# Norming the attention latents with tokens in the rows, and fixing TensorE's order, in a hybrid attention and convolution layer

## The chip, the cores and the metric

The kernel runs on one core of a Trainium2 chip. The metric is the device time of one execution in microseconds (us), the median over runs. One profiled execution gives the trace that the text reads. Engines are named as in the profile: PE is TensorE (PEld its weight loads), DVE is VectorE, ACT is ScalarE, POOL is GpSimd, and SP is SyncE, whose queue issues most of the DMAs.

## What is computed

One decoder layer on 256 tokens of 2048 float32 features. The input is normed, projected into ten parts, run through multi-head latent attention and a short gated convolution, and merged. The reference, cut to what matters here:

```python
h = _rmsnorm(x, pre_norm_g)
proj = jnp.einsum('bsd,de->bse', h, w_in)
(q_a, c_kv, k_rope, z_mla, c_in, b_gate, c_gate, z_conv,
 g_mla, g_conv) = jnp.split(proj, cuts, axis=-1)      # 512, 512, 64, then 2048 each

q = jnp.einsum('bsr,re->bse', _rmsnorm(q_a, q_a_norm_g), w_q_b)      # 16 heads of 128 + 64
kv = jnp.einsum('bsr,re->bse', _rmsnorm(c_kv, kv_a_norm_g), w_kv_b)  # 16 heads of 128 + 128
q_rope = _apply_rope(q_rope, cos, sin); k_rope = _apply_rope(k_rope, cos, sin)
attn = _causal_mla_attention(q_nope, q_rope, k_nope, k_rope, v)
y_mla = einsum(attn * silu(z_mla), w_o_mla)
u = c_gate * c_in; conv = causal 3-tap convolution of u
y_conv = einsum(b_gate * conv * silu(z_conv), w_o_conv)
merged = sigmoid(g_mla) * y_mla + sigmoid(g_conv) * y_conv
x = x + _rmsnorm(einsum(merged, w_out), post_norm_g)
```

`_rmsnorm(x, g)` is `x * rsqrt(mean(x*x) + eps) * g`. The norm of x is one factor per token, so the kernel projects the raw `x * g` and multiplies by that factor afterwards.

## The kernel before

**Numbers.** Every float32 operand of a large product is kept as a high and a low part in a matmul format (fp32r). ScalarE makes the high part (`split_act`, L211), VectorE the remainder (L212), and a product is taken as three matmuls: high x high, high x low, low x high. Where activations are the moving operand, high and low stand side by side in 512 columns (`halves`, L206: weight high times both; L208: weight low times the high 256). Where activations are stationary, `product` (L198 to L200) issues the three.

**Weights.** They come in units of 1 MB (128 x 2048), in the order of a list, `plan`. `load_raw` (L141) issues a unit on SyncE into one of three buffers `raw`; `split_unit` makes `whi` and `wlo` halves of 128 x 1024, five buffers each; `take(i)` splits one unit ahead and loads two more.

**Stages.** First the transposed input `xt` is loaded in pieces between the units of the q latent and split into `x_both` (L281, L282), which holds it with features in the rows for the whole kernel. The q latent (`qa`) takes four units and the four blocks of the c_kv latent (`ckv`) one each; both come out of TensorE with latent features in the rows and tokens in the columns, and `whole` (L329, L330) adds the two halves of a PSUM bank. Then comes the key's rope part (`kr`, L424). For the norms, `squares` squares on ScalarE (L293) and reduces on VectorE (L295), `rms_cols` sums over rows with a matmul against ones (L303), takes the power -1/2 on GpSimd (L310) and builds diagonal matrices (L314), and `rms_rows` spreads them over all rows with another matmul (L321). This is done for x, for q and for c_kv. `times_rows` and `latent_split` then scale and split. `tables` (L342 to L372) reduces the rotary angles on GpSimd in some 35 steps (L348 to L360, then pairs of L352 and L353), and VectorE and ScalarE make sine and cosine.

**Heads.** For each of 16 heads five projections of x follow, z, cg, ci, b and c (`project`), with the gates and the convolution, the scores after z (`scores`), the transposes of the softmax weights `p` after ci (`turn`, L522), the product with v after b (`values`), and, for the next pair of heads, `group_a` (query and key, after the first head of a pair) or `group_b` (query rope and v, after the second). In head 0 all groups, the scores, `turn` and `values` stand at the end. After the heads, four chunks of output columns: two gates, two products, a merge on VectorE (L655 to L660), and `features` (L633), which transposes the merged chunk with TensorE. The output product and the last norm end the kernel.

**Order.** The program runs under a tile scheduler that simulates the engines and picks, on each engine, the first ready instruction in program order; one that it thinks not ready may be passed by later ones. `tc.keep_in_program_order(i)` ties an instruction behind the one before it on its engine in the program.

Of the kernel before, what the change touches and what calls it, by code (L numbers as in the profile page):

```python
# [78 lines left out]
def tile_layer(ctx: ExitStack, tc: tile.TileContext, xt, x, pos, pvec, post_g, wqa, wi, wkr, wqk, wrv, wsq, out):  # L79
    nc = tc.nc  # L80

# [24 lines left out]
    u_qa = [add(wqa[k]) for k in range(4)]  # L106
    u_ckv = [add_wi() for _ in range(KR)]
# [87 lines left out]
    def product(ps, a, b, first, last):  # L195

        (ah, al), (bh, bl) = a, b
        nc.tensor.matmul(ps, ah, bh, start=first, stop=False)  # L198
        nc.tensor.matmul(ps, ah, bl, start=False, stop=False)  # L199
        nc.tensor.matmul(ps, al, bh, start=False, stop=last)  # L200

    def halves(blocks):


        for ps, w, both, first, _ in blocks:
            nc.tensor.matmul(ps[:, :], w[0], both, start=first, stop=False)  # L206
        for ps, w, both, _, last in blocks:
            nc.tensor.matmul(ps[:, :S], w[1], both[:, :S], start=False, stop=last)  # L208
# [24 lines left out]
    for _ in range(8):  # L233
        nc.tensor.matmul(idle[:, :P], ones[:, :], ones[:, :], start=True, stop=True)
# [4 lines left out]
    r_col = const.tile([P, LINE], F32, name="r_col")[:, :NT]  # L239
# [13 lines left out]
    kr = bp.tile([P, 2, S], F32R, name="kr")  # L253
    mask = bp.tile([P, 3 * P], F32, name="mask")
# [4 lines left out]
    xs = at_f  # L259
    angles = [at_f[:, H - 1 - i, :] for i in range(5)]  # L260
    lat_f = {"qa": cv_f[:, :KR, :], "ckv": cv_f[:, KR : 2 * KR, :]}
    sq_f = cv_f[:, 8:12, :]
    acc_f = {"x": cv_f[:, 12, :], "qa": cv_f[:, 13, :], "ckv": cv_f[:, 14, :]}
    row_f = at_f[:, 10, :]
    kr_f, kr_g = cv_f[:, 15, :], at_f[:, 9, :]
# [23 lines left out]
    def squares(name, chunks):  # L289

        acc = acc_f[name]
        for i, src in enumerate(chunks):
            nc.scalar.activation(sq_f, src, AF.Square)  # L293
            part = temp("f")[:, :] if i else acc
            nc.vector.reduce_sum(part, sq_f.rearrange("p k t -> p t k"), axis=mybir.AxisListType.X)  # L295
            if i:
                nc.vector.tensor_tensor(acc, acc, part, op=ALU.add)
        return acc

    def rms_cols(name, acc, width, r=None):  # L300
        ss = bank(f"ss_{name}", tag="sm", bufs=1)
        for t in range(NT):
            nc.tensor.matmul(  # L303
                ss[:, t : t + 1], acc[:, t * P : (t + 1) * P], ones[:, 0:1], start=True, stop=True
            )
        v = temp(f"v_{name}", (P, NT), tag="rms_v")
        nc.vector.tensor_scalar(v[:, :], ss[:, :NT], 1.0 / width, EPS, op0=ALU.mult, op1=ALU.add)
        if r is None:
            r = temp(f"r_{name}", (P, NT), tag="rms_r")
        nc.gpsimd.tensor_tensor(r[:, :], v[:, :], mhalf[:, :].to_broadcast([P, NT]), op=ALU.pow)  # L310
        dgs = []
        for t in range(NT):
            dg = temp(f"dg_{name}{t}", (P, P), tag=f"rms_d{t}", bufs=1)
            nc.vector.tensor_scalar(dg[:, :], ident[:, :], r[:, t : t + 1], None, op0=ALU.mult)  # L314
            dgs.append(dg)
        return dgs

    def rms_rows(name, dgs, r):
        rb = bank(f"rb_{name}", tag="sm", bufs=1)
        for t in range(NT):  # L320
            nc.tensor.matmul(rb[:, t * P : (t + 1) * P], ones[:, :], dgs[t][:, :], start=True, stop=True)  # L321
        nc.scalar.activation(r, rb[:, :S], AF.Copy)
        return r
# [18 lines left out]
    def tables():  # L342
        pi = angles[4].bitcast(I32)
        nc.scalar.dma_start(out=pi, in_=pos.to_broadcast([P, S]))
        y, n1, n2, r = angles[:4]
        v = nc.gpsimd
        nc.vector.tensor_copy(y[:, :], pi)
        v.tensor_scalar(r[:, :], y[:, :], col("freq"), None, op0=ALU.mult)  # L348

        def less(r, n, c):  # L350

            v.tensor_scalar(y[:, :], n[:, :], c, None, op0=ALU.mult)  # L352
            v.tensor_tensor(r[:, :], r[:, :], y[:, :], op=ALU.subtract)  # L353
# [3 lines left out]
        v.tensor_scalar(y[:, :], r[:, :], inv, None, op0=ALU.mult)  # L357
        v.tensor_scalar(n1[:, :], y[:, :], big, big, op0=ALU.add, op1=ALU.subtract)
        v.tensor_tensor(n2[:, :], y[:, :], n1[:, :], op=ALU.subtract)
        v.tensor_scalar(n2[:, :], n2[:, :], small, small, op0=ALU.add, op1=ALU.subtract)  # L360
        for w, c in TERMS:
            less(r, (n1, n2)[w], c)
        v.tensor_scalar(n1[:, :], r[:, :], inv, small, op0=ALU.mult, op1=ALU.add)
        v.tensor_scalar(n1[:, :], n1[:, :], small, None, op0=ALU.subtract)
        for c in COARSE:
            less(r, n1, c)
        lim = float(np.nextafter(np.float32(math.pi), np.float32(0)))
        nc.vector.tensor_scalar(r[:, :], r[:, :], lim, -lim, op0=ALU.min, op1=ALU.max)
        nc.vector.scalar_tensor_tensor(y[:, :], r[:, :], -1.0, r[:, :], op0=ALU.mult, op1=ALU.max)
        nc.scalar.activation(n2[:, :], r[:, :], AF.Sin)  # L370
        nc.scalar.activation(cos_t[:, :], y[:, :], AF.Sin, bias=hpi[:, :], scale=-1.0)
# [12 lines left out]
    def times_rows(dst):  # L384
        n = dst.shape[1]
        nc.vector.tensor_tensor(dst, dst, r_x[:, :].unsqueeze(1).to_broadcast([P, n, S]), op=ALU.mult)

    def latent_split(name, both, g, r):
        f = lat_f[name]
        for j in range(KR):  # L390
            nc.vector.scalar_tensor_tensor(
                f[:, j, :], f[:, j, :], col(g, j), r, op0=ALU.mult, op1=ALU.mult
            )
            split_act(both[:, j, :S], both[:, j, S:], f[:, j, :])

    pss = [bank(f"qa{j}") for j in range(KR)]
    for i in range(4):
        ahead(u_qa[i], split=0)
        for k in range(4 * i, 4 * i + 4):
            behind = split_scaled(x_both, xs[:, k, :], k)  # L400
        w = take(u_qa[i])
        for k4 in range(4):
            k = 4 * i + k4
            halves([(pss[j], w(k4 * KR + j, P), x_both[:, k, :], k == 0, k == KD - 1) for j in range(KR)])
    for j in range(KR):
        whole(lat_f["qa"][:, j, :], pss[j])
    with tc.issue_after(behind[0].ins), tc.issue_after(behind[1].ins):
        squares("x", [xs[:, 4 * i : 4 * i + 4, :] for i in range(4)])
    whole(lat_f["ckv"][:, 0, :], project(u_ckv[0], "ckv0", tag="tp", bufs=1))
    dg = rms_cols("x", acc_f["x"], D, r_col)  # L410
    whole(lat_f["ckv"][:, 1, :], project(u_ckv[1], "ckv1"))
    rms_rows("x", dg, r_x[:, :])
    times_rows(lat_f["qa"])
    squares("qa", [lat_f["qa"]])
    whole(lat_f["ckv"][:, 2, :], project(u_ckv[2], "ckv2"))
    whole(lat_f["ckv"][:, 3, :], project(u_ckv[3], "ckv3"))
    dg = rms_cols("qa", acc_f["qa"], R)
    times_rows(lat_f["ckv"])
    squares("ckv", [lat_f["ckv"]])
# [3 lines left out]
    for k in range(KD):  # L423
        nc.tensor.matmul(ps[:, :], w[k // 8][:, k % 8], x_both[:, k, :], start=k == 0, stop=k == KD - 1)  # L424
# [4 lines left out]
    latent_split("qa", qa, "q_g", rms_rows("qa", dg, row_f))  # L429
    tables()  # L430
# [31 lines left out]
    def group_b(g):  # L462
# [8 lines left out]
        for t in range(NT):  # L471
            ps = bank(f"vv{g}_{t}", **({} if g else {"tag": ("o", "tp")[t], "bufs": 1}))
# [6 lines left out]
    def scores(h):  # L479
# [5 lines left out]
        mm = nc.tensor.matmul  # L485
# [32 lines left out]
    def turn(h, p):  # L518

        tp = bank(f"tp{h}", tag="tp", bufs=1)  # L520
        for b in range(3):
            nc.tensor.transpose(tp[:, b * P : (b + 1) * P], p[:, b * P : (b + 1) * P], ident[:, :])  # L522
# [4 lines left out]
    def values(h, pt, sz):  # L527
# [5 lines left out]
        mm = nc.tensor.matmul  # L533
# [7 lines left out]
    def silu(name, ps):  # L541
        f, s = temp("sl_f", bufs=1), temp(name, bufs=1)
# [12 lines left out]
    for h in range(H):  # L555
        uz, ug, ui, ub, uc = u_head[h]
        sz = silu("sz", project(uz, f"z{h}"))
        if h == 0:
            dg_c = rms_cols("ckv", acc_f["ckv"], R)
            key_rope()  # L560
        else:
            p = scores(h)
# [3 lines left out]
        if h == 0:  # L566
            latent_split("ckv", ckv, "kv_g", rms_rows("ckv", dg_c, row_f))
# [5 lines left out]
        if h > 0:  # L573
            pt = turn(h, p)
        c = temp("c", bufs=1)
# [52 lines left out]
    def features(c, m):  # L628

        for t in range(NT):  # L630
            tp = bank(f"mt{c}_{t}", tag=("tp", "o")[t], bufs=1)
            for j in range(4):
                nc.tensor.transpose(tp[:, j * P : (j + 1) * P], m[t][:, j * P : (j + 1) * P], ident[:, :])  # L633
# [176 lines left out]
```

## Time and profile before

| | |
|---|---|
| median of 3 runs | 1073.79 us (1073.71 to 1073.86) |
| the profiled execution | 1074.65 us |
| its span in the trace | 1072.9 us |
| granted TensorE clock, mean | 0.995 |
| busy in the span: PE, PEld, DVE, ACT, POOL | 1054.6, 909.6, 728.8, 587.2, 48.0 us |
| moved by DMA | 199.80 MB, 186 GB/s in the mean |

Busy time is what the profiler shows per engine. Matmuls are pipelined, so one's length (about 390 ns for 512 columns) is more than the distance to the next (about 230 ns); distances are read from the starts. "Idle before" is the time in which an engine sat still before an instruction, and the name behind the arrow is what ended it.

### The profile page before, as it was taken

How to read it: one execution, taken by the hardware profiler on the slowest of the kernel's cores; microseconds unless marked ns; L12 is line 12 of the kernel's file. 1: busy time of each engine (PE TensorE's matmuls, PEld its weight loads, DVE VectorE, ACT ScalarE, POOL GpSimd, SP SyncE). 2: the span in 40 equal slices, each digit the busy share in tenths (PEclk: the TensorE clock that was granted, in tenths of full speed). 3: DMA queues.
4: the chain of work that ended last, by engine and by line, in shares of the span. 5: the costliest groups of instructions: out<-in, count | busy, mean ns of one | idle time of the engine just before them, and what ended most of it. 6: DMA issues, size and time to landing. Idle time of an engine off the chain costs nothing.

```text
span 1072.9 us, 14367 instructions
## 1 busy us (share of the span) xinstructions
PE 1054.6 (98%) x5576; PEld 909.6 (85%) x5576; DVE 728.8 (68%) x1132; ACT 587.2 (55%) x849; POOL 48.0 (4%) x70
## 2 busy tenths in 40 slices
PE   9989999999999999999999999999999999999997
PEld 7878798988988888889888878888888888888885
DVE  6899797777877878778787684454454445455562
ACT  7656566666666666666666664434434433434450
POOL 0591000000000000000000000000000000000000
PEclk9999999999999999999999999999999999999999
DMA  8644454454554545554545536555555555557552
GB/s 313 223 147 161 148 192 167 177 196 148 196 197 152 192 164 188 188 177 168 187 162 194 194 114 239 196 196 183 188 191 184 195 196 196 196 192 284 199 188 78
DMA packets 31604, 199.80 MB, mean 186 GB/s; under 512 B 3632, under 2 KB 5296, under 8 KB 9264
## 3 DMA queue, kind: packets, MB, share of 16 engines
q1 hardware_dynamic: 30960, 195.57, 51.8%
q10 hardware_dynamic: 576, 3.31, 0.8%
q8 instruction: 43, 0.70, 0.3%
q14 instruction: 25, 0.20, 0.1%
HBM read 196.78 MB, written 2.10 MB: 185 GB/s over the span
## 4 chain that ended last, share of the span: by engine, by line
PE 86%; DVE 5%; POOL 4%; issue 2%; DMA 2%; ACT 0%; SPq 0%; POOLq 0%; DVEq 0%; ACTq 0%
PE sq L199 10%; PE sq L200 10%; PE sq L198 10%; PE z L206 5%; PE cg L206 5%; PE ci L206 5%; PE c L206 5%; PE b L206 5%; PE c L208 3%; PE b L208 3%; PE z L208 3%; PE ci L208 3%; PE cg L208 3%; PE out L200 2%; PE out L198 2%
## 5 line engine op out<-in xcount | busy, mean ns | idle before, releaser
L212 DVE TENSOR_TENSOR wlo<-raw,whi 128x1024 fp32r<-128x1024 f32 (+1 forms) x372 | 442.6, 1205 | 230.2 <-ACT whi L211 192.7
L211 ACT ACTIVATE whi<-raw 128x1024 fp32r<-128x1024 f32 (+1 forms) x374 | 386.8, 1038 | 339.8 <-PE sq L200 181.3
L199 PE MATMUL sq<-wlo,x_both 128*128 128x512 f32 x256 | 99.7, 390 | 1.6 <-DVE wlo L212 1.6
L200 PE MATMUL sq<-whi,x_both 128*128 128x512 f32 x256 | 99.6, 389 | 0.0
L198 PE MATMUL sq<-whi,x_both 128*128 128x512 f32 x256 | 99.2, 390 | 0.0
L206 PE MATMUL z<-x_both,whi 128*128 128x512 f32 x256 | 62.7, 398 | 2.4 <-DVE f L330 2.4
L206 PE MATMUL ci<-x_both,whi 128*128 128x512 f32 x256 | 62.9, 398 | 0.0
L206 PE MATMUL b<-x_both,whi 128*128 128x512 f32 x256 | 62.2, 395 | 0.0
L206 PE MATMUL cg<-x_both,whi 128*128 128x512 f32 x256 | 61.3, 391 | 0.0
L206 PE MATMUL c<-x_both,whi 128*128 128x512 f32 x256 | 61.1, 391 | 0.0
L206 PEld LDWEIGHTS z<-x_both,whi 128*128 128x128 f32 x256 | 48.2, 193 | 12.2 <-issue 2.6
L199 PEld LDWEIGHTS sq<-wlo,x_both 128*128 128x128 f32 x256 | 48.1, 188 | 11.8 <-DVE wlo L212 2.0
L200 PEld LDWEIGHTS sq<-whi,x_both 128*128 128x128 f32 x256 | 48.1, 188 | 10.0
L198 PEld LDWEIGHTS sq<-whi,x_both 128*128 128x128 f32 x256 | 48.1, 188 | 9.9
L206 PEld LDWEIGHTS ci<-x_both,whi 128*128 128x128 f32 x256 | 48.0, 193 | 9.4
L206 PEld LDWEIGHTS c<-x_both,whi 128*128 128x128 f32 x256 | 47.0, 188 | 9.1
L206 PEld LDWEIGHTS cg<-x_both,whi 128*128 128x128 f32 x256 | 47.0, 188 | 9.1
L206 PEld LDWEIGHTS b<-x_both,whi 128*128 128x128 f32 x256 | 46.9, 188 | 9.1
L200 PE MATMUL out<-whi,m_both 128*128 128x512 f32 x128 | 49.9, 390 | 0.0
L198 PE MATMUL out<-whi,m_both 128*128 128x512 f32 x128 | 49.9, 390 | 0.0
L199 PE MATMUL out<-wlo,m_both 128*128 128x512 f32 x128 | 49.8, 389 | 0.0
L198 PE MATMUL sq<-whi,at_both 128*128 128x512 f32 x128 | 49.8, 389 | 0.0
(239 smaller groups left out, 1838.7 us busy)
## 6 DMA issues: line engine op xcount, KB each, us to landing
raw<-wi_dram SPq DMA_DIRECT2D x84, 1024.0 KB, 4.8
raw<-wsq_dram SPq DMA_DIRECT2D x80, 1024.0 KB, 4.8
raw<-wqk_dram SPq DMA_DIRECT2D x8, 1024.0 KB, 4.9
raw<-wrv_dram SPq DMA_DIRECT2D x8, 768.0 KB, 4.2
raw<-wqa_dram SPq DMA_DIRECT2D x8, 256.0 KB, 4.6
raw<-wqa_dram SPq DMA_DIRECT2D x4, 512.0 KB, 8.0
xr<-x_dram ACTq DMA_DIRECT2D x1, 2048.0 KB, 14.7
out_dram<-og SPq DMA_DIRECT2D x6, 256.0 KB, 2.3
```

The source lines that it names most:

```text
L198: nc.tensor.matmul(ps, ah, bh, start=first, stop=False)
L199: nc.tensor.matmul(ps, ah, bl, start=False, stop=False)
L200: nc.tensor.matmul(ps, al, bh, start=False, stop=last)
L206: nc.tensor.matmul(ps[:, :], w[0], both, start=first, stop=False)
L208: nc.tensor.matmul(ps[:, :S], w[1], both[:, :S], start=False, stop=last)
L211: nc.scalar.activation(hi, src, AF.Copy)
L212: nc.vector.tensor_tensor(lo, src, hi.bitcast(F32), op=ALU.subtract)
```

## The change

The q and c_kv latents are computed with `x_both` stationary and the weights moving, so that they come out with tokens in the rows, in two PSUM banks each. c_kv's weights are laid out like q's. The sum of squares of a token is then a sum along a row, which ScalarE's squaring gives along with it (`accum_out`); the squares of x come from a second load of x by tokens (`x_tok`, in the space of `cv_f`). `latent_norm` scales by tokens while it copies out of PSUM, and `latent_turn` transposes with TensorE and splits with the gain. Every matmul and transpose is kept in program order, as are the steps on GpSimd, the load by tokens, the squares of x and the two sines. The rotary tables are cut into three parts with the powers between, plus an end. In head 0 the order is like that of the other heads: groups earlier, scores after b, and `values` in head 1. The output gate `sz` gets a second buffer, and the first v products lie in the common banks.

```diff
+    def matmul(*a, **kw):
+        return tc.keep_in_program_order(nc.tensor.matmul(*a, **kw))
+    def transpose(*a):
+        return tc.keep_in_program_order(nc.tensor.transpose(*a))
...
-    u_qa = [add(wqa[k]) for k in range(4)]
-    u_ckv = [add_wi() for _ in range(KR)]
+    u_qa, u_ckv = ([add(wl[n, k]) for k in range(4)] for n in range(2))
...
-            order += [(h, 0), (h, 1), (h, 2), (h, 3), (h, 4), (0, "a"), (0, "b"), (1, "a")]
+            order += [(h, 0), (h, 1), (0, "a"), (h, 2), (0, "b"), (h, 3), (h, 4), (1, "a")]
...
         raws[i] = t
+        if i == u_ckv[1]:
+            tc.keep_in_program_order(nc.sync.dma_start(out=x_tok, in_=x))
...
+    lat_f = {n: at_f[:, 4 * i : 4 * i + 4, :].rearrange("p (t k) s -> p t (k s)", t=NT) for i, n in enumerate(("qa", "ckv"))}
+    kr_f, kr_g = at_f[:, 8, :], at_f[:, 9, :]
+    x_tok = cv_f[:, :, :].rearrange("p (t k) s -> p t (k s)", t=NT)
...
+        ss = temp(f"ss_{name}", (P, NT), tag="rms_s")
+        for t, (src, junk) in enumerate(chunks):
+            a = nc.scalar.activation(junk, src, AF.Square, accum_out=ss[:, t : t + 1])
+            if name == "x":
+                tc.keep_in_program_order(a)
+        return ss
+
+    def inverse_root(r, v):
+        tc.keep_in_program_order(
+            nc.gpsimd.tensor_tensor(r, v, mhalf[:, :].to_broadcast([P, NT]), op=ALU.pow)
+        )
+
+    def input_norm():
+        ss = squares("x", [(x_tok[:, t, :], x_tok[:, t, :]) for t in range(NT)])
+        v = temp("v_x", (P, NT), tag="rms_v")
+        nc.vector.tensor_scalar(v[:, :], ss[:, :], 1.0 / D, EPS, op0=ALU.mult, op1=ALU.add)
+        inverse_root(r_col[:, :], v[:, :])
+        nc.vector.tensor_tensor(r_sq[:, :], r_col[:, :], r_col[:, :], op=ALU.mult)
...
+    def input_rows(dgs):
+        rb = bank("rb", tag="sm", bufs=1)
+        for t in range(NT):
+            matmul(rb[:, t * P : (t + 1) * P], ones[:, :], dgs[t][:, :], start=True, stop=True)
+        nc.scalar.activation(r_x[:, :], rb[:, :S], AF.Copy)
...
+        yield
+        for i, (w, c) in enumerate(TERMS):
+            if i == 5:
+                yield
             less(r, (n1, n2)[w], c)
...
+    def tables_end():
...
+        tc.keep_in_program_order(nc.scalar.activation(n2[:, :], r[:, :], AF.Sin))
+        tc.keep_in_program_order(nc.scalar.activation(cos_t[:, :], y[:, :], AF.Sin, bias=hpi[:, :], scale=-1.0))
...
+    def latent_products(pss, k, w, wk):
+        cols = [x_both[:, k, o : o + P] for o in (0, P, S, S + P)]
+        wh, wl_ = w(wk, R)
+        for i, ws, first, last in ((0, wh, True, False), (2, wh, False, False), (0, wl_, False, True)):
+            for t in range(NT):
+                matmul(
+                    pss[t][:, :], cols[i + t], ws, start=first and k == 0, stop=last and k == KD - 1
+                )
+
+    def latent_norm(name, pss):
+        f = lat_f[name]
+        ss = squares(name, [(pss[t][:, :], f[:, t, :]) for t in range(NT)])
+        v, r = temp(f"v_{name}", (P, NT), tag="rms_v"), temp(f"r_{name}", (P, NT), tag="rms_r")
+        nc.vector.scalar_tensor_tensor(v[:, :], ss[:, :], 1.0 / R, r_sq[:, :], op0=ALU.mult, op1=ALU.mult)
+        nc.vector.tensor_scalar(v[:, :], v[:, :], EPS, None, op0=ALU.add)
+        inverse_root(r[:, :], v[:, :])
+        nc.vector.tensor_tensor(r[:, :], r[:, :], r_col[:, :], op=ALU.mult)
+        for t in range(NT):
+            nc.scalar.activation(f[:, t, :], pss[t][:, :], AF.Copy, scale=r[:, t : t + 1])
+
+    def latent_turn(name, both, g):
+        f = lat_f[name]
+        for j2 in range(2):
+            ps = bank(f"lt_{name}{j2}", tag=("tp", "o")[j2], bufs=1)
+            for j in range(2):
+                for t in range(NT):
+                    o, b = j * S + t * P, 2 * j2 + j
+                    transpose(ps[:, o : o + P], f[:, t, b * P : (b + 1) * P], ident[:, :])
+            for j in range(2):
+                b, src = 2 * j2 + j, ps[:, j * S : (j + 1) * S]
+                nc.scalar.activation(both[:, b, :S], src, AF.Copy, scale=col(g, b))
+                nc.vector.scalar_tensor_tensor(
+                    both[:, b, S:], src, col(g, b), both[:, b, :S].bitcast(F32), op0=ALU.mult, op1=ALU.subtract
+                )
...
+            latent_products(ps_q, 4 * i + k4, w, k4)
+    ps_c = [bank(f"ckv{t}") for t in range(NT)]
+    for i in range(4):
+        w = take(u_ckv[i])
+        for k4 in range(4):
+            latent_products(ps_c, 4 * i + k4, w, k4)
+        if i == 0:
+            table_parts = tables()
+            next(table_parts)
+        if i == 1:
+            dg = input_norm()
+            latent_norm("qa", ps_q)
+            next(table_parts)
...
+    input_rows(dg)
+    latent_norm("ckv", ps_c)
+    next(table_parts)
     whole(kr_f, ps)
...
         if h == 0:
-            dg_c = rms_cols("ckv", acc_f["ckv"], R)
-            key_rope()
+            latent_turn("qa", qa, "q_g")
         else:
+            if h == 1:
+                values(0, pt, sz0)
             p = scores(h)
         cg = temp("cg", bufs=1)
         whole(cg[:, :], project(ug, f"cg{h}"))
         rows(cg[:, :])
         if h == 0:
-            latent_split("ckv", ckv, "kv_g", rms_rows("ckv", dg_c, row_f))
+            latent_turn("ckv", ckv, "kv_g")
+            group_a(0)
...
         if h > 0:
             pt = turn(h, p)
+        else:
+            tables_end()
+            key_rope()
+            group_b(0)
...
         if h > 0:
             values(h, pt, sz)
             values_next(h)
+        else:
+            p = scores(h)
         sg = silu("sg", project(uc, f"c{h}"))
         nc.vector.tensor_tensor(cv_f[:, h, :], c[:, :], sg[:, :], op=ALU.mult)
         if h == 0:
-            group_a(0)
-            group_b(0)
-            p = scores(h)
             values_next(h)
-            values(h, turn(h, p), sz)
+            pt, sz0 = turn(h, p), sz
...
-                nc.tensor.transpose(tp[:, j * P : (j + 1) * P], m[t][:, j * P : (j + 1) * P], ident[:, :])
+                transpose(tp[:, j * P : (j + 1) * P], m[t][:, j * P : (j + 1) * P], ident[:, :])
```

More of the change, by code (lines that the diff above doesn't have):

```diff
@@ L197, in product @@
         (ah, al), (bh, bl) = a, b
[L198 to L200 removed]
+        matmul(ps, ah, bh, start=first, stop=False)
+        matmul(ps, ah, bl, start=False, stop=False)
+        matmul(ps, al, bh, start=False, stop=last)
     def halves(blocks):
         for ps, w, both, first, _ in blocks:
[L206 removed]
+            matmul(ps[:, :], w[0], both, start=first, stop=False)
         for ps, w, both, _, last in blocks:
[L208 removed]
+            matmul(ps[:, :S], w[1], both[:, :S], start=False, stop=last)
     def split_act(hi, lo, src):
@@ L233, in tile_layer @@
     for _ in range(8):
-        nc.tensor.matmul(idle[:, :P], ones[:, :], ones[:, :], start=True, stop=True)
+        matmul(idle[:, :P], ones[:, :], ones[:, :], start=True, stop=True)
     const.tile([P, LINE - 8], F32, name="const_pad")
@@ L238, in tile_layer @@
     r_x = const.tile([P, S], F32, name="r_x")
-    r_col = const.tile([P, LINE], F32, name="r_col")[:, :NT]
+    r_both = const.tile([P, LINE], F32, name="r_both")
+    r_col, r_sq = r_both[:, :NT], r_both[:, NT : 2 * NT]
     main = ctx.enter_context(ExitStack())
@@ L253, in tile_layer @@
     kr = bp.tile([P, 2, S], F32R, name="kr")
+    bp.tile([P, LINE], F32, name="bp_pad")
     mask = bp.tile([P, 3 * P], F32, name="mask")
@@ L289, in squares @@
     def squares(name, chunks):
[L291 to L310, printed above, removed]
+        ss = temp(f"ss_{name}", (P, NT), tag="rms_s")
@@ L397, in tile_layer @@
+    ps_q = [bank(f"qa{t}") for t in range(NT)]
     for i in range(4):
@@ L399, in tile_layer @@
         for k in range(4 * i, 4 * i + 4):
-            behind = split_scaled(x_both, xs[:, k, :], k)
+            split_scaled(x_both, xs[:, k, :], k)
         w = take(u_qa[i])
         for k4 in range(4):
[L403 to L419, printed above, removed]
+            latent_products(ps_q, 4 * i + k4, w, k4)
[11 more added lines that the diff above has]
+            next(table_parts)
     ahead(u_kr)
@@ L423, in tile_layer @@
     for k in range(KD):
-        nc.tensor.matmul(ps[:, :], w[k // 8][:, k % 8], x_both[:, k, :], start=k == 0, stop=k == KD - 1)
+        matmul(ps[:, :], w[k // 8][:, k % 8], x_both[:, k, :], start=k == 0, stop=k == KD - 1)
+    input_rows(dg)
+    latent_norm("ckv", ps_c)
+    next(table_parts)
     whole(kr_f, ps)
@@ L471, in group_b @@
         for t in range(NT):
-            ps = bank(f"vv{g}_{t}", **({} if g else {"tag": ("o", "tp")[t], "bufs": 1}))
+            ps = bank(f"vv{g}_{t}")
             for k in range(KR):
@@ L541, in silu @@
     def silu(name, ps):
-        f, s = temp("sl_f", bufs=1), temp(name, bufs=1)
+        f, s = temp("sl_f", bufs=1), temp(name, bufs=2 if name == "sz" else 1)
         whole(f[:, :], ps)
```

70 lines of the change are left out of this document (25 added, 45 removed).

## The prediction

> **What bounds the kernel now.** I read the page first, then TensorE's waits, then the timelines where it waits, and last the place where the tile scheduler has moved matmuls out of program order.
>
> The page's first two parts:
>
> ```profile
> PE 1054.6 (98%) x5576; PEld 909.6 (85%) x5576; DVE 728.8 (68%) x1132; ACT 587.2 (55%) x849; POOL 48.0 (4%) x70
> ...
> PE   9989999999999999999999999999999999999997
> ```
>
> TensorE (PE) is the bound from end to end. A change can only win by giving it less work, by closing its gaps, or by keeping its clock up. The gaps are few; TensorE's waits (total, times, longest) name them:
>
> ```profile
> PE rb_qa L321 <- DVE dg_qa L314: 2.8, 1, 2.8
> PE z L206 <- DVE f L330: 2.4, 1, 2.4
> PE sq L199 <- DVE wlo L212: 1.6, 1, 1.6
> ```
>
> The two longest lie in the prologue and first head, the part that the change rewrites. TensorE's timeline there (start, length, group, count, idle time before it and who ended it):
>
> ```profile
> 63.13 3.82 PE L206 MATMUL cg<-x_both,whi 128*128 128x512 f32 x16
> ...
> 71.61 1.05 PE L321 MATMUL rb_qa<-dg_qa,ones 128*128 128x128 f32 x4 [2.75 <-DVE dg_qa L314]
> 72.31 5.24 PE L206 MATMUL ci<-x_both,whi 128*128 128x512 f32 x16
> ...
> 111.99 5.48 PE L206 MATMUL z<-x_both,whi 128*128 128x512 f32 x16 [2.39 <-DVE f L330]
> ```
>
> After each gap the same sixteen matmuls take 5.24 and 5.48 us and not 3.82. The windows say why (clock and DMA are the columns before the last):
>
> ```profile
> 72.00:79.00 7.00, 7.00 (x34) 6.00 (x33) 6.52 (x11) 4.69 (x10) 6.41 (x8) 0.77 0.37 112
> 112.00:118.00 6.00, 6.00 (x22) 4.90 (x23) 4.76 (x11) 4.25 (x10) 0.00 (x0) 0.72 0.08 30
> 636.00:641.00 5.00, 3.41 (x16) 2.49 (x15) 5.00 (x8) 5.00 (x6) 0.00 (x0) 1.00 0.07 10
> ```
>
> The granted clock fell to 0.77 and 0.72 after idle stretches of 2.75 and 2.39 us; after 1.6 us at 640 it stayed at 1.00. So these gaps cost 1.4 and 1.7 us more than their length.
>
> GpSimd's timeline shows what is behind the first gap:
>
> ```profile
> 39.21 3.15 POOL L348 TENSOR_SCALAR at_f<-at_f,pv 128x256 f32<-128x256 f32 x1 [36.48 <-DVE at_f L347]
> ...
> 70.42 0.72 POOL L310 TENSOR_TENSOR r_qa<-v_qa,mhalf 128x2 f32<-128x2 f32 x1
> ...
> 83.32 1.23 POOL L310 TENSOR_TENSOR r_ckv<-v_ckv,mhalf 128x2 f32<-128x2 f32 x1
> 84.53 0.73 POOL L353 TENSOR_TENSOR at_f<-at_f 128x256 f32<-128x256 f32 x1
> ```
>
> The rotary tables occupy it without a pause from 39.21 to 85.26, and the small power steps of the norms queue between. The squares of x and the latents' norms also keep VectorE full (10.0 of 10 us in both 20:30 and 30:40). Its work piles up behind that until the scores of head 0 are released only after 112.
>
> **Matmul work.** The latents go from 64 matmuls of 512 columns plus 64 of 256 each to 96 of 512. The columns are the same. In the wide stages such matmuls start 0.227 us apart (974.61 to 976.65 for nine), so a latent takes 96 x 0.227 = 21.8 us. Now q takes 24.4 (5.36 to 29.77), of which 22.4 is sixteen times the 1.40 of one block (11.77 to 13.17) and 2.0 waits for the first loads. Those waits stay: unit 2 is released at 18.11 by its load, and only the eight blocks after it gain 0.04 each. So q gains about 0.45 and c_kv (22.3 now, four times 5.58) 0.55. The three column sums go (0.37 each: 45.05 to 45.42), and two of the three row broadcasts (0.70 and 0.44). Sixteen transposes come. Eight of the same shape take 0.87 us of TensorE (734.85, with the next two matmuls at 735.64 and 735.95 where 0.23 is usual), so sixteen cost 1.75. [...]
>
> **A walk through the new prologue**, with rows of before. Q ends at 29.3. C_kv: +21.8 = 51.1. Key rope: +3.65 = 54.7. Row broadcast: +0.5. Z of head 0 (5.57): 60.8. Turning q: +0.9 = 61.7. Cg: 67.3. Turning c_kv: 68.2. Group a (four narrow products, 1.40 each): 73.8. Ci: 79.4. Group b (1.40 + 24 x 0.119): 83.7. B: 89.2. Scores: 90.1. C: 95.7. Group a of the next pair: 101.3. Transposes of p: 101.6. Z of head 1: 107.2. Before, z of head 1 ends at 119.92, and its three p transposes are still to come (0.37). If nothing waits, the change is worth 13.0 us, 7 to 8 of it the gaps and low clocks above.
>
> **Where the covers are.** *Load by tokens:* 2 MB more, queued on SyncE behind the second c_kv weight unit (its buffer is free at 21.3), ahead of all later weights. The only such load in the trace took 14.7 us, so 36.4 at the latest. The third c_kv unit behind it then lands near 38 and is used at 40.2. Cost nothing, at most 2 us. *Squares of x:* ScalarE, two of 128x2048, 2 us each by the 1.04 of 1024; they follow the third unit's split, which waits for a weight buffer until 32, so they end at 38 to 41. *GpSimd:* its chain starts when position, load and at_f[15] are there. The old squares of x held at_f until 34.8; now the last split ends at 24.0, so I expect the start at 27 to 31. Five steps take 9.2 us (39.21 to 48.43), then the power for x (0.73), the one for q, five terms of 2.28 (eleven took 25.1 of queue), the one for c_kv, six terms, 2.5 and 6.3: tables ready near 78. *Key rope* needs a PSUM bank that q's scaled copy frees, near 46, needed at 51: 5 us of cover. *Latent c_kv* is normed by 56, turned at 67.3. *Group a:* kn needs the last turned block of c_kv; four ScalarE/VectorE pairs of 0.4 + 0.48, with weight splits of 1.06 and 1.23 between, end near 71.7 where kn's fourth product wants it near 71.5; I charge 0.5 (0 to 1.5). *Scores 0* need the tables, the sine (1.28 table load, pinned behind ci's evacuation at 80), key rope and query rope. In the trace clip to key split took 9.4 us, 6 of it other work in VectorE's queue; the same again for the query gives 89 to 92, against 89.5 wanted. I charge 1.0 (0 to 4). ScalarE and VectorE lose 6 reductions of 2.0 us, two 1.35 products and more, so I charge nothing else there.
>
> **TensorE in program order.** From head 2 on its stream is already in program order, but for four score matmuls slipped between two kn products in every other head. There the bank is free at 174.7 and wanted at 177.6: nothing. One place differs. The last chunk's transposes wait for VectorE's merge; before, the scheduler slipped 27 output matmuls in front:
>
> ```profile
> 976.65 0.39 PE L200 MATMUL sq<-whi,cv_both 128*128 128x512 f32 x1
> 976.88 0.39 PE L198 MATMUL out<-whi,m_both 128*128 128x512 f32 x1
> ...
> 980.06 0.60 PE L633 MATMUL mt<-ident,sg 128*128 128x128 f32 x4
> ```
>
> and VectorE meanwhile:
>
> ```profile
> 976.81 1.23 DVE L212 TENSOR_TENSOR wlo<-raw,whi 128x1024 fp32r<-128x1024 f32 x1 [1.03 <-ACT whi L211]
> 977.96 0.68 DVE L659 TENSOR_TENSOR sg<-sq,sg 128x512 f32<-128x512 f32 x1
> 978.67 0.69 DVE L660 TENSOR_TENSOR sg<-sg,sg 128x512 f32<-128x512 f32 x1
> ```
>
> In strict order the first four transposes go at 976.88 (their half is merged at 975.8), and the other four wait from 977.3 until 979.45, with every output matmul behind them: 2.2 us new (1.0 if the merge passes the weight split). By the nearest row, 2.39, the clock then falls too: 1.7 more (0 by the row of 1.6). [...]
>
> **Sum:** 13.0 - 0.5 - 1.0 - 2.2 - 1.7 = 7.6 us of gain, less 0.3 for small hand-overs in a rewritten stage: 7.3. The profiled span of 1072.9 becomes 1065.6. That execution took 1074.65, 0.86 above the median of 1073.79, and the median becomes 1066.5.
>
> **Rivals.** *A, the clock stays up and covers hold* (0.27): without the 1.7 and 1.0, 1062.5 to 1064.5. For it: 2.2 lies between a gap that dropped the clock and one that did not. *B, head 0 still waits* (0.14): tables or rope 3 to 5 us late for the scores, with a clock drop of 1.7: 1068 to 1071.5. For it: rope's steps stand in VectorE's queue among weight splits, and now nothing can pass the waiting score. *C, slower* (0.09): GpSimd's chain, now in fixed order, starts as late as before, because the cast of the positions lies behind other work in VectorE's queue. Starting at 39.2, the power for x ends near 49, q's copies at 53, key rope waits 2 us. The tables end at 86, the scores are released near 98 and wait 6 us more, plus 1.7 for the clock. That is 9.7, less the 1.0 charged: 1075.2. Decisive is a start later than about 40; each us after adds one. Against it: the old start was set by the squares, which no longer touch at_f. *D, the change does not do what it says* (0.02): the new gaps equal the old, 1072 to 1074.
>
> **Numbers.** Forecast 1066.5 (0.48, itself 1065 to 1068). The range 1061.5 to 1071.5 takes in A, B and the bounds and leaves out C and D. About 0.2% (2.1 us) is what a measurement of this kernel can tell from no change. Faster 0.87, within 0.04, slower 0.09.
>
> **What would show it.** Right: no TensorE wait over 2 us before 110; z of head 1 ending at 107 to 110; GpSimd starting before 32; a new wait of about 2 us at mt near 970 with a lower clock behind it; about 21.8 us per latent. Wrong: a wait of kr on q's copies, of sc on kr or qr over 3 us, TensorE waiting for a c_kv weight unit behind the token load, or new short waits in every head.

## The result: slower, by the order and not by the latents

| | before | after |
|---|---|---|
| median | 1073.75 us (1072.97 to 1073.86, 4 runs) | 1079.63 us (1078.96 to 1081.5, 4 runs) |
| profiled execution | 1074.65 us | 1079.21 us |
| its span, mean granted clock | 1072.9 us, 0.995 | 1077.4 us, 0.993 |

The ratio of after to before is 1.0056, with a 95% interval of 1.0044 to 1.0067. The forecast was 1066.5 us. The kernel became slower by 5.9 us.

The page of after, parts 1 and 2 (busy time of each engine; TensorE's busy tenths and granted clock in 40 slices of 27 us):

```profile
PE 1052.4 (98%) x5508; PEld 905.2 (84%) x5508; DVE 710.7 (66%) x1106; ACT 588.7 (55%) x850; POOL 47.7 (4%) x70
...
PE   8997999999999999999999989999999999999997
...
PEclk9998999999999999999999999999999999999999
```

TensorE has 68 matmuls less and VectorE 18 us less to do, as intended, and TensorE is still the bound. In the first slice the row falls from 9 to 8 (the waits for the first weight halves add up to 1.6 us for 1.0). There are two larger new dents: the fourth slice (81 to 108 us) is at 7, with the only clock digit below 9, and the slice from 620 us is at 8. TensorE's waits in after (total, times, longest) name them:

```profile
PE sc L84 <- DVE qr L220: 6.7, 1, 6.7
PE mt L87 <- DVE sg L706: 2.5, 1, 2.5
PE sq L84 <- DVE wlo L220: 2.2, 1, 2.2
PE kn L84 <- DVE ckv L436: 1.7, 2, 1.3
```

The waits of before at the row broadcast (2.8) and at z (2.4) are gone. In their place stand 6.7 at the scores of head 0 and 2.5 at mt, and the 1.6 at sq has grown to 2.2, with a smaller wait of 0.6 ahead of it.

Both traces, followed from place to place, make a ledger. It counts by how much after is ahead of before in the profiled executions; both start at 0.

| place | forecast: ahead by | measured |
|---|---|---|
| first matmul of the last stages, sq (624.11 before, 622.94 after) | 11.2 | 1.2 |
| first transpose mt (734.85, 736.69) | 11.2 | -1.8 |
| end of TensorE (1065.04, 1069.53) | 7.3 | -4.5 |

Ten of the twelve microseconds that are missing were lost in the prologue and head 0, three at 640 us, and the term at mt was the only one charged too high (3.9 against 2.7).

**Where the prologue lost it.** TensorE's timeline in after (start, length, group, count, idle time before it and who ended it):

```profile
72.67 0.49 PE L84 MATMUL kn<-ckv,whi 128*128 128x512 f32 x1 [0.42 <-DVE ckv L436]
74.47 0.97 PE L84 MATMUL kn<-ckv,whi 128*128 128x512 f32 x3 [1.31 <-DVE ckv L436]
...
77.13 3.82 PE L84 MATMUL ci<-x_both,whi 128*128 128x512 f32 x16
...
92.54 0.28 PE L84 MATMUL sc<-kn,qn_hi 128*128 128x256 f32 x1
92.65 0.22 PE L84 MATMUL sc<-kn,qn_lo 128*128 128x128 f32 x1
99.59 0.58 PE L84 MATMUL sc<-kr,qr 128*128 128x256 f32 x1 [6.72 <-DVE qr L220]
...
101.04 5.18 PE L84 MATMUL c<-x_both,whi 128*128 128x512 f32 x16
```

Against the walk of the forecast, with its charge of 0.5, ci starts 2.8 us late (77.13 for 74.3). From ci to the scores it is exact (15.41 for 15.4). From the scores to c it takes 8.50 for 1.9, and c itself takes 6.93 (101.04 to 107.97) for 5.57. Until 99.59 nothing else runs on TensorE, although the products of c and of the next pair of heads need nothing of these scores. The windows say what the idle stretch did to the clock, and what VectorE did meanwhile (columns: busy time and count of PE, PEld, DVE, ACT, POOL, then granted clock, DMA share, GB/s):

```profile
93.00:99.00 6.00, 0.00 (x0) 0.00 (x0) 5.89 (x12) 0.83 (x3) 0.10 (x1) 0.84 0.48 172
99.00:105.00 6.00, 5.41 (x18) 4.61 (x19) 3.15 (x12) 3.32 (x8) 0.00 (x0) 0.59 0.22 89
```

VectorE was busy for 5.89 of the 6 us in which TensorE did nothing. Its timeline shows the operand that TensorE waits for, and what stands ahead of it:

```profile
85.25 0.34 DVE L392 TENSOR_SCALAR sin_t<-at_f,pv 128x256 f32<-128x256 f32 x1
...
92.80 1.71 DVE L400 TENSOR_TENSOR rp_b<-f,sin_t 32x256 f32<-32x256 f32 x4
...
94.88 1.22 DVE L220 TENSOR_TENSOR wlo<-raw,whi 128x1024 fp32r<-128x1024 f32 x1
...
96.41 1.22 DVE L220 TENSOR_TENSOR wlo<-raw,whi 128x1024 fp32r<-128x1024 f32 x1
...
99.12 0.87 DVE L220 TENSOR_TENSOR qr<-f,qr 64x256 fp32r<-64x256 f32 x2
```

The tables are ready at 85.6. The query rope's last step ends at 99.99, 14.4 us later. Its own steps take 3.8 of that. The rest is other work: four weight halves (wlo, 4.9) that the next products want, the key's rope (3.0), and the epilogues of c, b and v.

**Where the last stages lost it.** After 640 us (TensorE's timeline and window, both of after):

```profile
635.94 0.50 PE L84 MATMUL sq<-whi,x_both 128*128 128x512 f32 x1 [0.57 <-ACT whi L219]
638.59 0.50 PE L84 MATMUL sq<-wlo,x_both 128*128 128x512 f32 x1 [2.15 <-DVE wlo L220]
```

```profile
640.00:646.00 6.00, 6.00 (x21) 4.83 (x20) 3.68 (x4) 2.12 (x2) 0.00 (x0) 0.73 0.82 340
```

Before has one wait of 1.59 here, and its clock stays at 1.00 in this window:

```profile
640.00:646.00 6.00, 6.00 (x27) 4.94 (x28) 4.62 (x5) 2.12 (x4) 0.00 (x0) 1.00 0.82 318
```

From the first of these matmuls to the long wait, before runs 62 and after 55: the scheduler had moved seven ahead, six of the second half of the tokens and one of a later product, and they filled 1.6 us of the time in which VectorE caught up. In program order they stand behind the wait, TensorE idles for 2.72, and the clock falls to 0.73.

### The profile page after: what moved, and what is told of

Same layout as the page of the kernel before. It is cut to its first block, busy times and chain, and to the rows that moved or that the text cites. A ratio compares the mean times of both kernels' runs of the same rounds, so it can differ in the third digit from the quotient of the medians.

```text
span 1077.4 us, 14193 instructions
## 1 busy us (share of the span) xinstructions
PE 1052.4 (98%) x5508; PEld 905.2 (84%) x5508; DVE 710.7 (66%) x1106; ACT 588.7 (55%) x850; POOL 47.7 (4%) x70
## 4 chain that ended last, share of the span: by engine, by line
PE 92%; DVE 4%; issue 1%; DMA 1%; ACT 0%; SPq 0%; POOLq 0%; POOL 0%; DVEq 0%; ACTq 0%
PE sq L84 31%; PE c L84 8%; PE z L84 8%; PE ci L84 8%; PE cg L84 8%; PE b L84 8%; PE out L84 7%; PE kn L84 2%; PE ckv L84 2%; PE vv L84 2%; PE qn L84 2%; PE sc L84 1%; DVE wlo L220 1%; DMA raw<-wl_dram 1%; PE qa L84 1%
## 5 line engine op out<-in xcount | busy, mean ns | idle before, releaser
L84 PE MATMUL sq<-whi,x_both 128*128 128x512 f32 x512 | 160.6, 392 | 0.6 <-ACT whi L219 0.6
L84 PE MATMUL sq<-whi,cv_both 128*128 128x512 f32 x256 | 79.5, 389 | 0.0
L84 PE MATMUL sq<-whi,at_both 128*128 128x512 f32 x256 | 79.5, 389 | 0.0
L84 PE MATMUL out<-whi,m_both 128*128 128x512 f32 x256 | 79.1, 389 | 0.0
L84 PEld LDWEIGHTS out<-whi,m_both 128*128 128x128 f32 x256 | 48.1, 188 | 10.0
L84 PEld LDWEIGHTS sq<-whi,at_both 128*128 128x128 f32 x256 | 48.0, 188 | 10.0
L84 PEld LDWEIGHTS sq<-whi,cv_both 128*128 128x128 f32 x256 | 48.0, 188 | 10.0
## 6 DMA issues: line engine op xcount, KB each, us to landing
cv_f<-x_dram SPq DMA_DIRECT2D x1, 2048.0 KB, 12.2
```

Of the source, the lines that this page charges most:

```text
L84: return tc.keep_in_program_order(nc.tensor.matmul(*a, **kw))
```

## Experiments

Theory 1: the fixed order of TensorE costs all of it, and the rest of the change is worth what the forecast gave. Its rivals: the tables are too late (GpSimd), or the scores of head 0 stand too early in the program. Every edit is against the kernel after unless it says otherwise.

**pe_free**: nothing is tied on TensorE; all else stays, the rewritten latents and the new order of head 0 in the program too.

```diff
     def matmul(*a, **kw):
-        return tc.keep_in_program_order(nc.tensor.matmul(*a, **kw))
+        return nc.tensor.matmul(*a, **kw)
     def transpose(*a):
-        return tc.keep_in_program_order(nc.tensor.transpose(*a))
+        return nc.tensor.transpose(*a)
```

> The changed kernel with TensorE's fixed order taken back: no matmul and no transpose is tied, all else stays. Theory 1 (the fixed order is what costs: in three places TensorE may no longer pass an instruction that waits): the wait before the scores of head 0 (6.7 us, and some 2 us of low clock behind it) is filled with head 0's c and later products, the wait at 640 goes from 2.7 back to about 1.6 us with a clock of 1.00, the one at mt (2.5) goes; the time is 1079.6 - 8 - 2.7 - 2.5, that is 1066 to 1069. Theory 2 (rope and tables come too late in the new prologue, and nothing else is ready for TensorE then): only the two late places recover and the time is 1074 to 1075.

Measured: 1063.98 us (1063.67 to 1064.22), a ratio to before of 0.9911 (0.9896 to 0.9926). That is 15.7 us less than after, and 2 us below the range that was expected. TensorE's waits in it, and the timeline at the place of the 6.7:

```profile
PE qa L84 <- ACT whi L219: 2.1, 3, 1.1
PE sq L84 <- DVE wlo L220: 1.4, 1, 1.4
PE kn L84 <- DVE ckv L436: 1.0, 1, 1.0
```

```profile
84.52 0.28 PE L84 MATMUL sc<-kn,qn_hi 128*128 128x256 f32 x1
84.64 0.23 PE L84 MATMUL sc<-kn,qn_lo 128*128 128x128 f32 x1
...
91.75 3.82 PE L84 MATMUL c<-x_both,whi 128*128 128x512 f32 x16
...
103.47 3.35 PE L84 MATMUL z<-x_both,whi 128*128 128x512 f32 x14
106.65 0.28 PE L84 MATMUL sc<-kr,qr 128*128 128x256 f32 x1
```

The scores are the most telling part. The query rope ends even later than in after (103.47), and the first rotary score goes 22 us behind the two that begin the group. It costs nothing, because c, the next pair's products and most of z of head 1 run in between. In the six microseconds behind the wait at sq (630:636 in this run) and in the six behind the last mt (973:979) the clock is 1.00. VectorE is no less full than in after (9.92 of the 10 us from 90 to 100), so the gain doesn't come from a shorter queue there. In the ledger pe_free is 10.5 us ahead of before at the first sq (613.65), 10.7 at the first mt and 10.5 at the end of TensorE: it loses neither the ten microseconds of the prologue nor anything at the two late places. Theory 1 holds, and this version beats both kernels.

**tail_free**: only two late stretches are untied, that is all products of the first gate (sq) and the output products of the first of four column blocks (early).

```diff
-    def product(ps, a, b, first, last):
+    def product(ps, a, b, first, last, mm=matmul):
...
-    product(pss[t][:, :], a, w(k4, 512), k == 0, k == KD - 1)
+    product(pss[t][:, :], a, w(k4, 512), k == 0, k == KD - 1,
+            nc.tensor.matmul if (c, n) == (0, 0) else matmul)
...
-    def out_products(ps, t, w, kk):
+    def out_products(ps, t, w, kk, early=False):
...
-                out_products(pss[t], t, w, kk)
+                out_products(pss[t], t, w, kk, c == 0)
```

> The changed kernel with only two stretches of matmuls untied: the first gate's products (the sq matmuls from about 623 on) and the first third of the output products. Theory 1: the wait at 640 falls from 2.7 to about 1.6 us and its clock stays at 1.00 (together 2.7 us), the wait of 2.5 at mt goes; 1079.6 - 5.2 is 1074.4 (1073.5 to 1075.5), with the wait of 6.7 before the scores of head 0 unchanged. Rival (VectorE's queue sets these two waits, whatever TensorE does meanwhile): 1078 to 1080.

Measured: 1073.6 us (1071.97 to 1076.85), ratio 1.0001 (0.9991 to 1.001), so 6.0 less than after. The wait at mt is gone, that at 640 is back to 1.4 and its clock to 1.00; the 6.7 at the scores stays. From the first sq to the end of TensorE it is 0.2 us faster than before, where after is 5.7 slower. So the remaining 9.6 us to pe_free lie ahead of the first sq, which fits the ten of the ledger.

**few_terms**: fewer steps on GpSimd, to see whether the tables set the wait.

```diff
-TERMS = [(w, c) for m, w, c in sorted(_terms, reverse=True) if m > 2.0**-29]
+TERMS = [(w, c) for m, w, c in sorted(_terms, reverse=True) if m > 2.0**-29][:6]
```

> The changed kernel with 6 of the 11 terms of the angle reduction on GpSimd (the angles are less exact), so that its chain ends some 11 us earlier, near 70. If the tables on GpSimd set the wait before the scores of head 0, it falls from 6.7 by 4 us or more, and the run is near 1073. If VectorE's queue and the sine's place behind ci set it (the sine ran right behind ci's evacuation at 83.4 and the query rope ended 14.7 us after it), the wait stays at 5.5 to 7 and the run is within 1.5 us of 1079.6.

Measured: 1081.66 us in one run. GpSimd's last step ends at 70.5 instead of 81.6, eleven microseconds sooner, and the wait at the scores is still 6.7, as the second expectation has it. The time is half a microsecond above that expectation, and in this execution the clock also fell behind the waits at kn (to 0.75; 1.00 in after). The end of the tables on GpSimd is not what sets this wait.

**few_terms_early**: as few_terms, and the end of the tables and the key rope are traced right behind group a, ahead of ci.

```diff
             latent_turn("ckv", ckv, "kv_g")
             group_a(0)
+            tables_end()
+            key_rope()
...
         else:
-            tables_end()
-            key_rope()
             group_b(0)
```

> few_terms (6 of 11 terms of the angle reduction, TensorE tied; 1081.7 in its one time) with the sines and the key rope traced before ci of head 0 instead of behind it. few_terms showed that the tables' end is not what sets the wait before the scores. If the place of the sines and the 13 to 15 us of VectorE's queue behind them set it, the sines now run near 78 and not 87, the query rope is ready near 92 and the wait falls from 6.7 to under 2 us: 1071 to 1074. If the weight splits fill whatever time there is, the wait stays above 4: 1077 to 1081.

Measured: 1077.74 us (1075.74 to 1079.61), ratio 1.0033 (1.0023 to 1.0043). The sine table comes 3.6 us sooner (81.66), the query rope ends only 2 us sooner (97.95), and the wait is 4.5. That is the second expectation: the wait stays above 4. From the sine table's end to the rope's end it is now 15.9 us for 14.4, with six weight halves of 1.2 us between for the four of after: what is made ready sooner waits longer in VectorE's queue.

**scores_late**: order fixed, but the scores of head 0 stand behind c in the program, their turn behind z of head 1, and head 0's values behind cg of head 1.

```diff
             if h == 1:
-                values(0, pt, sz0)
+                pt0 = turn(0, p0)
             p = scores(h)
...
+        elif h == 1:
+            values(0, pt0, sz0)
...
             values(h, pt, sz)
             values_next(h)
-        else:
-            p = scores(h)
         sg = silu("sg", project(uc, f"c{h}"))
...
         if h == 0:
+            p0, sz0 = scores(h), sz
             values_next(h)
-            pt, sz0 = turn(h, p), sz
```

> The changed kernel, all orders fixed, with the scores of head 0 traced after its c projection instead of before it, its transposes of p after z of head 1, its values after cg of head 1. Theory 1: the query rope is ready near 100 as before, c (5.6 us) now runs before it, and the wait falls from 6.7 to 1 or 2 us and with it the low clock: 1079.6 - 7.5 is 1072 (1071 to 1073.5). Theory 2: the rope's steps slip as far behind in VectorE's queue as the scores do, the wait stays above 4 us: 1077 to 1079.

Measured: 1076.09 us (1074.71 to 1077.68), ratio 1.0024 (1.0014 to 1.0034): 3.5 us gained. The result lies between the two expectations: the wait is not gone but 3.0, since the query rope slipped to 102.93. Its trace also has the same wait at mt as after (it ends at 978.65 here and at 981.83 in after), and the clock there differs (window of scores_late, then of after, whose next stretch, 982:988, is at 1.00 too):

```profile
980.00:986.00 6.00, 6.00 (x21) 4.74 (x21) 0.63 (x1) 0.97 (x1) 0.00 (x0) 0.73 0.99 419
```

```profile
980.00:986.00 6.00, 4.17 (x21) 3.55 (x22) 3.51 (x5) 1.50 (x2) 0.00 (x0) 1.00 1.01 416
```

**free_late**: scores_late and pe_free together.

> TensorE untied as in pe_free, with the scores of head 0 traced later as in scores_late. With the order fixed that was worth 3.5 us. Theory 1: a free scheduler already passes the waiting scores, so the place in the program is worth nothing: within 1 us of 1064.0. Rival: the earlier trace still costs something by its priority on VectorE and ScalarE: 1061 to 1062.5.

Measured: 1063.71 us (1063.43 to 1064.47), ratio 0.9903 (0.9887 to 0.992). The same as pe_free within their spread: where the scores stand in the program is worth nothing that can be measured once TensorE is free to pass them.

**free_old_head**: pe_free with head 0 in the order of before (group a, group b, scores, turn and values all at its end).

> TensorE untied as in pe_free (1064.0), and head 0 back in the old order: its groups, scores, transposes and values at its end, its weight units in the old places; the latents in rows, the load by tokens and the tied steps on GpSimd stay. If the new order of head 0 carries the gain, the old wait of 2.4 us before z of head 1 and its 1.7 us of low clock come back: 1068 to 1070. If the latents and their norms carry it (the wait of 2.75 for rb_qa with its clock gone, VectorE relieved), the scheduler fills the rest: 1064 to 1066.5.

Measured: 1066.67 us (1066.09 to 1066.81), ratio 0.9929 (0.9914 to 0.9943). That is just above the second expectation. So with TensorE free the new order of head 0 is worth about 3 us (2.7 against pe_free, 3.0 against free_late), and the latents, norms and squares about 7 (1073.55, the kernel before measured beside it, less 1066.67).

**before_pinned**: the kernel before, with every matmul and transpose tied as in after.

> The kernel before with nothing changed but that every matmul and transpose is tied in program order. Theory 1 (the fixed order costs wherever the program has a waiting instruction ahead of ready ones): the waits at 640 and mt appear here too (about 2.7 and 2.5 us), and in the prologue each norm's small matmuls now hold up the projections traced behind them, and head 0's chain of scores, transposes and values runs bare: 1085 to 1110. If a fixed order alone is harmless and the loss belongs to the rewritten head 0: 1073 to 1078.

Measured: 1095.5 us in one run, about 22 more than before, as Theory 1 had it. Its longest waits on TensorE:

```profile
PE ss_x L83 <- DVE cv_f L303: 7.1, 1, 7.1
PE sc L83 <- DVE qr L218: 5.8, 1, 5.8
PE rb_ckv L83 <- DVE dg_ckv L320: 2.7, 1, 2.7
PE mt L86 <- DVE sg L666: 2.5, 1, 2.5
```

The kernel before had the late query rope too, and the same wait at mt. Its stream had hidden them.

**rope_first**: order fixed; VectorE's part of head 0's b projection, its weight halves included, is queued behind the query rope's last step.

```diff
...
-            group_b(0)
+            rope_end = group_b(0)
...
+        if h == 0:
+            with tc.issue_after(rope_end.ins):
+                ps_b = project(ub, "b0")
+        else:
+            ps_b = project(ub, f"b{h}")
-        whole(b[:, :], project(ub, f"b{h}"))
+        whole(b[:, :], ps_b)
```

> The changed kernel, order fixed, with one thing more: on VectorE the weight splits and other steps traced with head 0's b projection are queued behind the query rope's last step. Before this, six weight halves (7 us) stood between the sine and that step. If that queue is what makes the rope late, the last step ends near 93 to 94 and not 100, the wait before the scores falls from 6.7 to 1 or 2 us, the low clock behind it goes, and the time is 1071 to 1073.5. Rival (the splits are needed just as much, and the wait turns up at b or c instead): 1077 to 1080.

Measured: 1079.99 us (1079.73 to 1081.18), ratio 1.0051 (1.0034 to 1.0068). Nothing gained. The query rope ends at 94.6, 5.4 us sooner, and the scores wait 1.1. (Between the sine and the rope's last step of after stood four weight halves, 4.9 us, and not six; here there is none.) But TensorE's waits show a new one, and VectorE's timeline its cause (both of rope_first):

```profile
PE tp L87 <- DVE p L557: 6.5, 1, 6.5
...
PE sc L84 <- DVE qr L220: 1.1, 1, 1.1
```

```profile
93.71 0.87 DVE L220 TENSOR_TENSOR qr<-f,qr 64x256 fp32r<-64x256 f32 x2
94.61 5.77 DVE L220 TENSOR_TENSOR wlo<-raw,whi 128x1024 fp32r<-128x1024 f32 x5
```

Five weight halves that were put off now run in a row ahead of the softmax, and the transposes of p wait instead of the scores. As the rival said, the splits are needed just as much, though the wait turned up at p and not at b or c. The wait is VectorE's backlog; it moved, with its size.

**fixed_mended**: tail_free, rope_first and scores_late together, the order otherwise fixed.

> TensorE's order still fixed everywhere but in the two stretches of tail_free; rope_first and scores_late added. Theory 1 in its strong form (the three waits are the whole loss, and the fixed order is harmless elsewhere): 1079.6 - 6.0 (tail_free as measured) - 8.9 (the wait before the scores with its clock) is 1064.7, as good as pe_free's 1064.0 (1063.5 to 1066.5). Rival (a fixed order also loses in many places too small to be listed): 1067 to 1070.

Measured: 1071.78 us (1069.8 to 1074.45), ratio 0.9975 (0.9965 to 0.9986). Better than before by 0.25%, but 7.8 us short of pe_free and slower than both expectations: 3.3 of waiting is left at tp, 1.7 at kn and 1.4 at z, and the window 110:120 is at a clock of 0.83. The loss isn't spread over many small places, as the rival had it: in the profiled executions pe_free is 8.5 us ahead of fixed_mended when b of head 1 begins (122.16 against 130.71) and 7.6 at the end. Three repairs of the written order don't make what the freely ordered stream makes.

## Why the prediction was wrong

**The part that was right.** Without its step on program order, the forecast was a gain of 13.0 - 0.5 - 1.0 - 0.3 = 11.2 us, from 1074.65 to 1063.4 for the profiled execution. pe_free, which is the change without that step, has 1064.17. Its z of head 1 ends at 109.7, in the "107 to 110" given. That the sum fits so closely is in part luck: the walk let head 0 run in program order, and pe_free gets there by leaving that order. A latent takes 21.76 us for 21.8 (29.61 to 51.37), eight transposes 0.79 for 0.87 (lt_qa starts at 61.02, cg at 61.81). GpSimd starts its chain at 28.30, for 27 to 31. After five steps it stands still for 6.5 us until the squares of x come (they end at 42.2, for 38 to 41), and the tables end at 81.6, for 78; by few_terms this cost nothing. So rival C, the only one on the slow side, had the sign right and the mechanism wrong:

```profile
28.30 2.81 POOL L355 TENSOR_SCALAR at_f<-at_f,pv 128x256 f32<-128x256 f32 x1 [25.56 <-DVE at_f L360]
```

**The step that failed: "TensorE in program order".** It said that "one place differs", and priced mt alone. Three things were wrong with it.

*Its question was too narrow.* It compared the orders from head 2 on, where the program and the stream were the same, and treated the rewritten part as a walk in program order "if nothing waits". before_pinned shows what a free stream had been hiding: 22 us. The sign stood in the trace that the prediction read (TensorE, then VectorE, both of before):

```profile
102.36 0.63 PE L208 MATMUL qr<-qa,wlo 128*128 128x256 f32 x4
...
106.12 0.39 PE L487 MATMUL sc<-kn,qn_hi 128*128 128x256 f32 x1 [0.32 <-DVE kn L212]
...
118.62 0.28 PE L489 MATMUL sc<-kr,qr 128*128 128x256 f32 x1
```

```profile
114.14 0.87 DVE L212 TENSOR_TENSOR qr<-f,qr 64x256 fp32r<-64x256 f32 x2
```

The first scores of head 0 go at 106.12 and the rotary ones at 118.62; between them lie two kn products and most of z of head 1. The query's product ended at 102.8 and its rope at 115.0, 12.2 us later. That row is nearer than the key's 9.4 us that the prediction used. Laid on the walk, where the query's product ends at 80.8, it gives 93.0, and scores that wait 3.5 us instead of 1.0.

*The term for the scores of head 0, "1.0 (0 to 4)", was mis-sized.* It measured 6.72, and about 2 us more for the lowered clock (c took 1.4 more, the rest of the scores 0.7). Rival B named just this, "now nothing can pass the waiting score", and had 0.14 and 3 to 5 us. What made it larger: the walk counted the cover of each operand by itself, and charged "nothing else" for VectorE, since its total falls. But a total over the kernel says nothing of one stretch. VectorE is busy in 9.81 of the 10 us from 90 to 100, and TensorE in 3.28. In pe_free VectorE is as full (9.92) and TensorE is busy in all ten: the free stream gives VectorE time by running matmuls whose operands are ready, the fixed one doesn't.

*640 was not seen.* The claim that the last stages stood in program order but for mt missed the seven matmuls that the scheduler had moved there. Price: 3.0 us, of them 1.1 of waiting (2.72 for 1.59) and the rest with a clock of 0.73.

**Smaller terms.** kn's wait for the turned c_kv was charged 0.5 (0 to 1.5) and is 1.7; with the half of lt_ckv that waited 0.6, ci starts 2.8 late by the walk. The 0.45 that q was to gain don't follow from eight blocks of 0.04 each (0.3), and the trace has 0.2 (q ends at 29.61, for 29.77 in before). Rival B's own terms, 3 to 5 of waiting less the 1.0 charged and 1.7 for the clock, give 1070.2 to 1072.2 and not 1068 to 1071.5. The wait at mt was charged 2.2 and is 2.5. The clock after it was charged 1.7 and in the profiled run cost 0; in scores_late and before_pinned it did fall, to 0.72, after the same wait.

## What to carry to other kernels

Before an engine's order is fixed, count every place where its stream leaves program order now, in the stages that the change rewrites too: each may be a late operand that other work hides, and a fixed order turns it into idle time and, at times, a slower clock behind it (in after 6.72 us at the scores of head 0, with 0.59 in the window 99:105; 2.50 us at mt, with 1.00). Ask for the time between a late operand's inputs and its end in the trace of before, and which engine's queue it stands in; if that engine is full in this stretch, an edit that brings one operand forward may only move the wait to the next, as in rope_first (from 6.7 us to 1.1 at the scores, and 6.5 new at the transposes of p). Where a change holds a rewrite and a fixed order, they are two changes and want two prices: here the rewrite alone saved 10 us (1063.98 against 1073.75 and 1074.02) and the fixed order cost 15.7. The second price depends on the rest of the program: in the kernel before, the same fixing cost about 22 in its one run.

## What was not expected of the hardware

In these runs the clock did not follow the length of the idle stretch alone. The clocks here are those of the 6 us behind the stretch, in the profiled executions:

| place | idle | clock behind it |
|---|---|---|
| mt, six runs | 2.49 or 2.50 us | 1.00 in after, few_terms, few_terms_early and rope_first; 0.72 in scores_late and before_pinned |
| sq near 640, the six runs that tie it | 0.57, then 2.15 or 2.16 | 0.72 to 0.76 in all six |
| kn in head 0, five runs | 0.40 to 0.42, then 1.30 or 1.31 | 1.00 in after, rope_first and fixed_mended; 0.72 in tail_free and scores_late |
| kn, the two runs with fewer terms | 1.24 to 1.28, then 0.95 or 0.96 | 0.75 in few_terms, 1.00 in few_terms_early |
| single stretches in the prologue and head 0 | 2.39 and 2.75; 2.42 and 2.70 | 0.72 after both in before; 1.00 after both in before_pinned |
| single stretches, seven runs | 1.37 to 1.72 | 1.00 in all |

So a clock of 0.72 stands behind 1.3 us of idling that came shortly after a first pause of 0.4 (tail_free, scores_late), and one of 1.00 behind a single stretch of 2.70 (before_pinned). The drop at kn cost 1.6 us in tail_free: from the second kn wait's end to the end of ci it takes 9.8 us, in after 8.2. Of the rows, only that of the single stretches of 1.37 to 1.72 us has 1.00 throughout. What decides where a row is mixed was not shown.

The runs also scatter more where such gaps are left: after spreads over 2.5 us in 4 runs and tail_free over 4.9 in 10, pe_free over 0.6 in 4. That the gaps are the reason is argued from these spreads and was not tried by itself.
